# Feed-forward activations: PE transposes replaced by VectorE block transposes and a trip through memory, in a one-core trunk layer

## The chip, the cores and the metric

One core of a Trainium2 chip runs the whole program. The metric is the device time of one launch in microseconds (us); smaller is better. The engines are named as the profile names them: PE (TensorE), ACT (ScalarE), DVE (VectorE), POOL (GpSimd) and SP (SyncE, which here only issues DMAs). SBUF is the working memory, PSUM the accumulators that PE writes.

## The reference

One layer on 256 tokens with width 2048: a norm, an input projection, two mixers (an RWKV-7 recurrence and a gated delta rule), an output projection with a residual, and a gated feed-forward with width 5632. The change touches the feed-forward alone:

```python
x = x + y @ w_out[l]
h = rms_norm(x, ffn_norm_w[l])
x = x + (jax.nn.silu(h @ ffn_w_gate[l]) * (h @ ffn_w_up[l])) @ ffn_w_down[l]
return rms_norm(x, final_norm_w)
```

Everything is float32.

## The kernel before, in words

**Numbers in two halves.** A float32 product is made of three passes of a faster format: each operand is split into a rounded high part and the remainder (`wh` and `wl` for weights, the two halves of `h` for activations), and the passes are high x high, high x low, low x high. ACT makes the high part by a copy (L197 for weights, L241 for activations), DVE the low part by a subtraction (L198, L242).

**The feed-forward by units.** The 44 column blocks of the feed-forward are taken four at a time: eleven units, numbered 0, 4, 8 to 40 after their first block. For each unit there is a *gate* (`gate`, 128 token rows by 512 columns for both halves of the tokens, 96 matmuls, L1065), an *up* of the same size, and two halves of a *down* (`down`, 48 matmuls each, L1142). Gate and up leave their result with tokens on the partitions (`sg`, two tiles of 128 x 512, product at L1084). Down needs the activations with features on the partitions, so they are turned: `turn` does it with eight PE transposes of 128 x 128 into two PSUM tiles (L1097) and then splits these into `h`.

**Order of a unit.** In the loop over units c and the next one c1, the kernel writes gate(c1), down(c, 0), up(c1), down(c, 1); the transposes of c1 stand in the middle of down(c, 1). So `h` of c1 is ready one gate ahead of its use in down(c1, 0).

**Weights.** Every 512 KB of weights is one `load_split` (L179): SP issues the DMA into one of three `raw` buffers, ACT and DVE split it in two halves of 512 columns into one of two `wh` and two `wl` buffers, and PE uses it in 12 matmuls. A gate or an up has eight such loads, a half of a down four. The last unit's down weights come early through `raw_end` and the `wend` places.

**What sets the order.** The code is written in program order, with the feed of the matmuls marked as high priority, and a scheduler with a timeline of its own makes one list of instructions for each engine; each engine then goes through its list in order. `together` ties instructions into a given order. A DMA signals its landing on one of eight semaphores, which are handed out in turn; a DMA whose semaphore is still in use waits for that earlier DMA to land.

Of the kernel before, what the change touches and what calls it, by code (L numbers as in the profile page):

```python
# [17 lines left out]
P = 128  # L18
# [31 lines left out]
def trunk_kernel(ctx, tc, xT, vecs, fnw, w_up, a_up, g_up, w_in, w_ab, w_out, w_gu, w_dn, out):  # L50
# [9 lines left out]
    def hi():  # L60
        return tc.high_priority(offset=HI)
# [81 lines left out]
    class Side:  # L143
# [4 lines left out]
        def step(self):  # L148
            if self.cond is not None:
                if not self.cond():  # L150
                    return False
                self.cond = None
            try:
                self.cond = next(self.gen)
            except StopIteration:
                self.done = True
                side.remove(self)
            return True
# [8 lines left out]
            assert any([g.step() for g in list(side)])  # L167


    first = []  # L170

    def load_split(src, by_k=False, whole=False):

        with hi():
            if first:
                raw = first.pop(0)
            else:
                raw = wp.tile([P, 1024], F32, tag="raw", name="raw", bufs=RAW)
                SY.dma_start(out=raw.rearrange("p (c f) -> p c f", c=4) if by_k else raw, in_=src)  # L179
            wh = wp.tile([P, 1024], F32R, tag="wh", name="wh", bufs=WH)  # L180
            wl = wp.tile([P, 1024], F32R, tag="wl", name="wl", bufs=WL)
            both = [(wh[:, h * 512:h * 512 + 512], wl[:, h * 512:h * 512 + 512]) for h in range(2)]
            if whole:
                split(wh, wl, raw)
                return both
            it = iter(both)
            return halves_of(raw, lambda: next(it), by_k)
# [51 lines left out]
    def split(hi_ap, lo_ap, src, scale=None):  # L239
        if scale is None:  # L240
            S.activation(hi_ap, src, AF.Copy)  # L241
            V.tensor_tensor(lo_ap, src, hi_ap, ALU.subtract)  # L242
        else:
            S.activation(hi_ap, src, AF.Copy, scale=scale)
            V.scalar_tensor_tensor(lo_ap, src, scale, hi_ap, ALU.mult, ALU.subtract)
# [825 lines left out]
    def gate(c0, beside=None):  # L1071
        banks = gate_up(c0, 0, beside=beside)
        sg = [fp.tile([P, 512], F32, tag="tg", name="sg", bufs=2) for _ in range(2)]
        with hi():
            for tb in range(2):
                S.activation(sg[tb], banks[tb], AF.Silu, scale=rstd2[:, tb:tb + 1])
        last_gate[0] = sg[1]
        return sg

    def up(c0, sg, tag="pb"):  # L1080
        banks = gate_up(c0, 1, tag)
        with hi():
            for tb in range(2):
                V.scalar_tensor_tensor(sg[tb], banks[tb], rstd2[:, tb:tb + 1], sg[tb], ALU.mult, ALU.mult)  # L1084
        return sg

    def turn(c0, sg, before=()):

        h = act.tile([P, 4, 2 * T], F32R, tag="act", name=f"h{c0}")
        ps, ms = [], []  # L1090
        for b in range(2):
            ps.append(mps("psT", ("mr", "mc", "mg")[nbank[0] % 3]))
            nbank[0] += 1
            for i in range(2):
                for tb in range(2):
                    o = i * T + tb * P
                    ms.append(PE.transpose(ps[b][:, o:o + P], sg[tb][:, (2 * b + i) * P:(2 * b + i) * P + P], ident))  # L1097
        together([*before, *ms])
        for b in range(2):
            with hi():  # L1100
                p3, hs = ps[b].rearrange("p (i t) -> p i t", i=2), slice(2 * b, 2 * b + 2)
                split(h[:, hs, 0:T], h[:, hs, T:], p3)
        return h

    nbank = [0]

    def wend_slots():

        one = ["lw", "SB", "sq2", "bk", "i3"] + ["kt", "rt"] * 2 + ["vt"] * 4
        bufs = {"kt": 2, "rt": 2, "vt": 4}  # L1110

        def places():
            x2w = rp.tile([P, 8, 512], F32R, tag="AT1", name="wend")
            for i in range(8):
                yield x2w[:, i, :]
            w = act.tile([P, 4, 2 * T], F32R, tag="act", name="wend")
            for i in range(4):
                yield w[:, i, :]
            w = rp.tile([P, 2, 512], F32R, tag="Yt", name="wend")
            yield w[:, 0, :]  # L1120
            yield w[:, 1, :]
            for t in one:
                yield rp.tile([P, 512], F32R, tag=t, name="wend", bufs=bufs.get(t, 1))
            for i in range(6):
                yield fp.tile([P, 512], F32R, tag=("wend", "sq2")[i // 4], name="wend", bufs=(4, 2)[i // 4])
        g = places()
        return lambda: (next(g), next(g))
# [35 lines left out]
            S.copy(acc[:, tb, (q0 + q) * 512:(q0 + q) * 512 + 512], ps[q])  # L1163

    sg = gate(units[0], turn_x2)
    h = turn(units[0], up(units[0], sg, "mg"))

    for c, c1 in zip(units, units[1:]):
        sg = gate(c1)
        down(c, h, 0)  # L1170
        up(c1, sg)
        ahead = []
        down(c, h, 1, lambda m: ahead.append(turn(c1, sg, [m])))
        h = ahead[0]


    n = 4
# [110 lines left out]
```

## Time and profile before

| | |
|---|---|
| median of 3 runs | 1256.41 us (1255.57 to 1258.25) |
| the profiled execution's own time | 1257.04 us |
| its span, first to last instruction | 1255.3 us |
| PE busy | 1231.5 us, 98% of the span |
| DVE, ACT busy | 835.0 us (67%), 650.4 us (52%) |
| feed-forward gate and up matmuls (L1065, high weights) | 1408 matmuls, 377.4 us |
| PE transposes of the activations (L1097) | 88, eight for each of eleven units |
| DMA queue of SP | 171328 packets, 222.19 MB, 60.7% of 16 engines |

Rows of the profile read like this: line, engine, operation, what is written from what, the shapes, how many, then busy time and the mean duration of one, then how long the engine sat idle just before and what ended that idle time. For matmuls the busy time overlaps from one to the next. The chain of waits is followed back from the last instruction; in its list in order of time each piece has its start and its length in us. For a DMA issue the duration is the time for which SP is occupied; the time to landing runs from the start of the issue.

### The profile page before, as it was taken

The page shows a single profiled execution, that of the slowest core. Times are in us where ns is not written, and L with a number is a line of the kernel's source. Part 1 is how long each engine was busy: PE and PEld are TensorE (multiplying, and loading weights), DVE is VectorE, ACT ScalarE, POOL GpSimd, SP SyncE. Part 2 cuts the span into 40 slices and gives each one's busy share as a digit, 9 for nine tenths or more (in the row PEclk, how much of TensorE's full clock was granted, in tenths as well). Part 3 has the DMA queues.
Part 4 walks back from the last instruction along what each step waited for, and adds up shares of the span by engine and source line. Part 5 has one row for each costly group of instructions (what it writes and reads, how often), then busy time and mean ns, then how long its engine had stood idle before and what let it go on. Part 6 is the DMA issues. An engine that isn't in the chain of part 4 may idle for free.

```text
span 1255.3 us, 21107 instructions
## 1 busy us (share of the span) xinstructions
PE 1231.5 (98%) x8122; PEld 1084.1 (86%) x8122; DVE 835.0 (67%) x1634; ACT 650.4 (52%) x1199; POOL 17.0 (1%) x63
## 2 busy tenths in 40 slices
PE   7999999999999999999999999999999999999997
PEld 6999999999999989888888888888888888878886
DVE  7987887978966867555556555655656565665554
ACT  6665555666545556664444444444444444454443
POOL 3000000000000000000000000000000000000000
PEclk9999999999999999999999999999999999999999
DMA  6555666575573445676666666766666766676651
GB/s 232 167 168 178 162 170 157 168 183 142 179 231 118 135 165 188 167 209 191 190 191 195 188 190 194 197 188 197 186 187 189 194 187 195 202 239 192 194 150 67
DMA packets 175701, 226.68 MB, mean 181 GB/s; under 512 B 52272, under 2 KB 144560, under 8 KB 175344
## 3 DMA queue, kind: packets, MB, share of 16 engines
q1 hardware_dynamic: 171328, 222.19, 60.7%
q10 hardware_dynamic: 4128, 2.10, 0.6%
q8 instruction: 64, 1.05, 0.4%
q0 software_dynamic: 144, 1.05, 0.2%
q14 instruction: 37, 0.30, 0.1%
HBM read 218.75 MB, written 4.46 MB: 178 GB/s over the span
## 4 chain that ended last, share of the span: by engine, by line
PE 86%; DMA 5%; DVE 5%; ACT 1%; SPq 1%; issue 1%; DVEq 0%; ACTq 0%
PE psq L1065 36%; PE psd L1142 17%; PE psb L215 16%; PE psb L218 8%; DMA raw_end<-in_w_dn 2%; DVE wl L242 1%; PE psT L1097 1%; DMA raw<-in_w_in 1%; DMA A_r<-sA 1%; DMA sA<-AT 1%; PE psd L1193 1%; PE psd L1191 1%; PE psd L1192 1%; PE ps_A L480 1%; DVE wend L198 1%
## 5 line engine op out<-in xcount | busy, mean ns | idle before, releaser
L198 DVE TENSOR_TENSOR wl<-raw,wh 128x512 fp32r<-128x512 f32 x524 | 341.5, 694 | 273.0 <-ACT wh L197 271.0
L197 ACT ACTIVATE wh<-raw 128x512 fp32r<-128x512 f32 x524 | 302.0, 625 | 363.2 <-PE psq L1065 203.9
L1065 PE MATMUL psq<-wh,x2s 128*128 128x512 f32 x1408 | 377.4, 390 | 0.4 <-ACT wh L197 0.4
L1065 PEld LDWEIGHTS psq<-wh,x2s 128*128 128x128 f32 x1408 | 263.7, 188 | 55.6 <-ACT wh L197 1.0
L1065 PE MATMUL psq<-wl,x2s 128*128 128x512 f32 x704 | 217.2, 389 | 0.0
L215 PE MATMUL psb<-xs,wh 128*128 128x256 f32 x816 | 207.3, 288 | 7.6 <-ACT wh L197 6.1
L218 PE MATMUL psb<-xs,wh 128*128 128x256 f32 x816 | 206.9, 287 | 0.0
L1142 PE MATMUL psd<-wh,h 128*128 128x512 f32 x640 | 203.5, 391 | 1.0 <-ACT wh L197 1.0
L241 ACT ACTIVATE wh<-raw 128x1024 fp32r<-128x1024 f32 x128 | 135.3, 1057 | 86.6 <-PE psb L218 71.2
L215 PEld LDWEIGHTS psb<-xs,wh 128*128 128x128 f32 x816 | 157.3, 193 | 9.1 <-ACT wh L197 6.1
L242 DVE TENSOR_TENSOR wl<-raw,wh 128x1024 fp32r<-128x1024 f32 x128 | 155.9, 1218 | 10.8 <-ACT wh L241 10.7
L218 PEld LDWEIGHTS psb<-xs,wh 128*128 128x128 f32 x816 | 157.4, 193 | 1.5 <-issue 0.7
L1065 PEld LDWEIGHTS psq<-wl,x2s 128*128 128x128 f32 x704 | 132.0, 188 | 27.5
L1142 PEld LDWEIGHTS psd<-wh,h 128*128 128x128 f32 x640 | 119.1, 188 | 26.3 <-ACT wh L197 2.3
L215 PE MATMUL psb<-xs,wl 128*128 128x256 f32 x816 | 127.8, 287 | 2.2 <-DVE wl L198 1.2
L1142 PE MATMUL psd<-wl,h 128*128 128x512 f32 x320 | 124.6, 389 | 0.0
L215 PEld LDWEIGHTS psb<-xs,wl 128*128 128x128 f32 x816 | 110.4, 193 | 4.5 <-DVE wl L198 2.0
L1142 PEld LDWEIGHTS psd<-wl,h 128*128 128x128 f32 x320 | 60.1, 188 | 12.7
L218 PE MATMUL psb<-ys,wh 128*128 128x256 f32 x256 | 64.5, 288 | 2.5 <-DVE ys L242 2.5
L215 PE MATMUL psb<-ys,wh 128*128 128x256 f32 x256 | 64.7, 289 | 0.2 <-ACT ys L241 0.2
L218 PEld LDWEIGHTS psb<-ys,wh 128*128 128x128 f32 x256 | 50.1, 196 | 2.8 <-DVE ys L242 2.7
L1150 DVE TENSOR_TENSOR acc<-acc,psd 128x512 f32<-128x512 f32 x80 | 49.5, 681 | 1.8 <-PE psd L1142 1.8
(312 smaller groups left out, 1014.2 us busy)
## 6 DMA issues: line engine op xcount, KB each, us to landing
raw<-in_w_gu SPq DMA_DIRECT2D x176, 512.0 KB, 4.8
raw<-in_w_in SPq DMA_DIRECT2D x99, 512.0 KB, 3.9
raw<-in_w_dn SPq DMA_DIRECT2D x80, 512.0 KB, 4.2
raw<-in_w_out SPq DMA_DIRECT2D x32, 512.0 KB, 3.5
raw_end<-in_w_dn SPq DMA_DIRECT2D x8, 512.0 KB, 4.4
xraw<-in_xT SPq DMA_DIRECT2D x8, 256.0 KB, 6.3
x<-in_xT SPq DMA_DIRECT2D x1, 2048.0 KB, 9.7
raw<-in_w_ab SPq DMA_DIRECT2D x2, 512.0 KB, 6.1
```

The costliest lines, as they stand in the source:

```text
L197: S.activation(oh, src, AF.Copy)
L198: V.tensor_tensor(ol, src, oh, ALU.subtract)
L215: PE.matmul(ps[:, 0:T], w, rt[:, ri, 0:T], start=(first and k == 0 and not low), stop=(last and k == 7 and low == 1))
L218: PE.matmul(ps[:, 0:T], w, rt[:, ri, T:], start=False, stop=False)
L241: S.activation(hi_ap, src, AF.Copy)
L242: V.tensor_tensor(lo_ap, src, hi_ap, ALU.subtract)
L480: PE.matmul(psA[h][:, ch, :], bk[hr, ch].rearrange("p a t -> p (a t)"), ar[hr, p, ch].rearrange("p a t -> p (a t)"), start=True, stop=True)
L1065: last = PE.matmul(banks[tb], t[:, ri, o + tb * P:o + tb * P + P], w, start=(k == 0 and o == 0 and w is wh), stop=(k == KB - 1 and w is wl))
L1097: ms.append(PE.transpose(ps[b][:, o:o + P], sg[tb][:, (2 * b + i) * P:(2 * b + i) * P + P], ident))
L1142: m = PE.matmul(banks[tb * 2 + cg], st, parts[cg][w], start=(i == 0 and w == 0 and st is hh), stop=(i == n - 1 and st is hl))
L1150: V.tensor_tensor(acc[:, tb, cs], acc[:, tb, cs], banks[tb * 2 + cg], ALU.add)
L1191: PE.matmul(ps, hh, wh, start=(i == 0), stop=False)
```

## The change

For units 0 to 36 the activations no longer go through PE. A new function, `turn_far`, transposes each `sg` tile in blocks of 32 x 32 on DVE (`V.transpose`) into `tn`. What is then still wrong is where the blocks lie. `tn` is stored to a tensor in memory, `sH`, with two DMAs of 256 KB, and read back with sixteen DMAs of 32 KB, each for 32 partitions and one column block, in runs of 128 bytes, into the low half of `h`; then ACT and DVE split it in place. The three steps (store, read, split) are called from the next unit's gate, after its second, fourth and sixth weight load; the sixteen reads are tied behind the last weight load issued by then and to each other. Unit 40, the last, keeps the PE transposes, in the middle of down as before. One small buffer (tag `i3`) moves from the end's places to `tn`.

```diff
-    first = []
+    first, loads = [], []
...
-                SY.dma_start(out=raw.rearrange("p (c f) -> p c f", c=4) if by_k else raw, in_=src)
+                loads.append(SY.dma_start(out=raw.rearrange("p (c f) -> p c f", c=4) if by_k else raw, in_=src))
...
+    def turn_far(c0, sg):
+
+        tn = []
+        for tb in range(2):
+            tn.append(rp.tile([P, 512], F32, tag=("i2", "i3")[tb], name=f"tn{tb}"))
+            with hi():
+                V.transpose(tn[tb], sg[tb])
+        h = act.tile([P, 4, 2 * T], F32R, tag="act", name=f"h{c0}")
+        sH = dr.tile([2, 4, 32, 512], F32, name=f"sH{c0}")
+        raw = h[:, :, T:].bitcast(F32)
+        blocks = sH.rearrange("b a r (i q c) -> q r i (b a) c", i=4, q=4)
+
+        def step(i, last):
+            with hi():
+                if i == 0:
+                    for tb in range(2):
+                        SY.dma_start(out=sH[tb].rearrange("a r f -> (a r) f"), in_=tn[tb])
+                elif i == 1:
+                    together([loads[-1]] + [SY.dma_start(out=raw[q * 32:q * 32 + 32, j].rearrange("r (a c) -> r a c", c=32),
+                                                         in_=blocks[q][:, j]) for q in range(4) for j in range(4)])
+                elif i == 2:
+                    split(h[:, :, 0:T], h[:, :, T:], raw)
+        return h, step
...
-        one = ["lw", "SB", "sq2", "bk", "i3"] + ["kt", "rt"] * 2 + ["vt"] * 4
+        one = ["lw", "SB", "sq2", "bk"] + ["kt", "rt"] * 2 + ["vt"] * 4
...
-    h = turn(units[0], up(units[0], sg, "mg"))
+    h, step = turn_far(units[0], up(units[0], sg, "mg"))
 
     for c, c1 in zip(units, units[1:]):
-        sg = gate(c1)
+        sg = gate(c1, step)
         down(c, h, 0)
         up(c1, sg)
-        ahead = []
-        down(c, h, 1, lambda m: ahead.append(turn(c1, sg, [m])))
-        h = ahead[0]
+        if c1 != units[-1]:
+            ahead = [turn_far(c1, sg)]
+            down(c, h, 1)
+        else:
+            ahead = []
+            down(c, h, 1, lambda m: ahead.append((turn(c1, sg, [m]), None)))
+        h, step = ahead[0]
```

The order of the instructions on the engines moves with it. On SP, in the changed kernel, from the four loads of a down half of unit 4 on, through the gate in which unit 8's activations are read back (`sH_8118` is their place in memory, `h_8117` the tile they are read into):

```order
L179 DMA raw<-in_w_dn 128x1024 x4
L1121 DMA sH_8118<-tn_8113 128x512
L179 DMA raw<-in_w_gu 128x4x256
L1121 DMA sH_8118<-tn_8115 128x512
L179 DMA raw<-in_w_gu 128x4x256 x3
L1123 DMA h_8117<-sH_8118 32x8x32 x7
L179 DMA raw<-in_w_gu 128x4x256
L1123 DMA h_8117<-sH_8118 32x8x32 x5
L179 DMA raw<-in_w_gu 128x4x256
L1123 DMA h_8117<-sH_8118 32x8x32 x4
L179 DMA raw<-in_w_gu 128x4x256 x2
```

Before, the same stretch was four loads of the down half and eight of the gate with nothing between them. Now the two stores stand ahead of the gate's first and second load, and the reads behind its fourth, fifth and sixth. A part of the same list again, with what each DMA waits for (`DMAHW2` is one of the eight landing semaphores, `DVE` the raw buffer coming free), from the gate's fifth load on:

```order
L179 DMA raw<-in_w_gu 128x4x256 [waits DMAHW2_49,DVE_49]
L1123 DMA h_8117<-sH_8118 32x8x32 [waits DMAHW3_49]
L1123 DMA h_8117<-sH_8118 32x8x32 [waits DMAHW4_49]
L1123 DMA h_8117<-sH_8118 32x8x32 [waits DMAHW5_49]
L1123 DMA h_8117<-sH_8118 32x8x32 [waits DMAHW6_49]
L1123 DMA h_8117<-sH_8118 32x8x32 [waits DMAHW7_49]
L179 DMA raw<-in_w_gu 128x4x256 [waits DMAHW0_49,DVE_49]
L1123 DMA h_8117<-sH_8118 32x8x32 [waits DMAHW1_49]
L1123 DMA h_8117<-sH_8118 32x8x32 [waits DMAHW2_49]
```

Each waits for the DMA eight places back: the fifth load for the fourth load's landing, and the fourteenth read, the last row, for the fifth load's.

On DVE, before, from the product of unit 8's up to the end of the next gate's first split (`h_8135` is that unit's tile, read from PSUM):

```order
L1084 SCALAR_TENSOR_TENSOR sg<-psq,rstd_6748,sg 128x512 x2
L198 TENSOR_TENSOR wl<-raw,wh 128x512 x6
L242 TENSOR_TENSOR h_8135<-psT,h_8135 128x2x256 x2
L198 TENSOR_TENSOR wl<-raw,wh 128x512 x2
L1150 TENSOR_TENSOR acc<-acc,psd 128x512 x4
```

and now:

```order
L1084 SCALAR_TENSOR_TENSOR sg<-psq,rstd_6748,sg 128x512 x2
L198 TENSOR_TENSOR wl<-raw,wh 128x512
L1111 STREAM_TRANSPOSE tn_8113<-sg 128x512
L198 TENSOR_TENSOR wl<-raw,wh 128x512
L1111 STREAM_TRANSPOSE tn_8115<-sg 128x512
L198 TENSOR_TENSOR wl<-raw,wh 128x512 x6
L1174 TENSOR_TENSOR acc<-acc,psd 128x512 x4
L198 TENSOR_TENSOR wl<-raw,wh 128x512 x8
L242 TENSOR_TENSOR h_8117<-h_8117 128x4x256
L198 TENSOR_TENSOR wl<-raw,wh 128x512 x16
```

The two transposes follow the product, between half splits of weights. The split of `h`, once in down, now stands in the gate: the eight half splits ahead of it are those of the gate's second to fifth load, and the first behind it is the sixth load's. ACT has the same place for its part:

```order
L1076 ACTIVATE sg<-psq,rstd_6748 128x512 x2
L197 ACTIVATE wh<-raw 128x512 x38
L241 ACTIVATE h_8117<-h_8117 128x4x256
L197 ACTIVATE wh<-raw 128x512 x10
L1076 ACTIVATE sg<-psq,rstd_6748 128x512 x2
```

Before, this list had 28 weight halves, two splits of `h` from PSUM, and 20 halves; now 38 halves, one split of `h`, and 10.

## The prediction

> **What bounds the kernel now.** First the page: busy shares and the chain of work that ended last.
>
> ```profile
> PE 1231.5 (98%) x8122; PEld 1084.1 (86%) x8122; DVE 835.0 (67%) x1634; ACT 650.4 (52%) x1199; POOL 17.0 (1%) x63
> PE 86%; DMA 5%; DVE 5%; ACT 1%; SPq 1%; issue 1%; DVEq 0%; ACTq 0%
> ```
>
> PE is busy 98% of the span and holds 86% of the chain. So the feed-forward stage runs at the pace of its matmuls, and work taken off PE there is worth its full time, as long as PE gets its operands. The chain in order of time, over one unit, shows how little else is in it:
>
> ```profile
> 681.36 5.44 PE psd L1142 x24
> 686.80 0.87 PE psT L1097 x8
> 687.68 5.47 PE psd L1142 x24
> 693.15 21.76 PE psq L1065 x96
> 714.91 10.88 PE psd L1142 x48
> ```
>
> A gate takes 21.76 us for 96 matmuls and 8 weight loads, so one load feeds 12 matmuls, 2.72 us. The eight transposes of a unit take 0.87 us, as bare PE time. The gate that starts at 693.15 is my sample; its loads are numbered 0 to 7 and times are given from its start. Load 5 is wanted at 5 x 2.72 = 13.60.
>
> What supplies PE is one strict line: SP issues a load into one of three raw buffers, ACT rounds it, DVE subtracts.
>
> ```profile
> 692.45 0.37 SPq L179 DMA_DIRECT2D raw<-in_w_gu  x1
> 696.05 0.37 SPq L179 DMA_DIRECT2D raw<-in_w_gu  x1
> 697.44 0.37 SPq L179 DMA_DIRECT2D raw<-in_w_gu  x1
> ...
> raw<-in_w_gu SPq DMA_DIRECT2D x176, 512.0 KB, 4.8
> ```
>
> These are the issues of loads 3, 4 and 5: -0.70, +2.90 and +4.29. An issue occupies SP for 0.37, and 4.8 us after its start the load has landed.
>
> **What is removed.** Ten units lose their transposes (the eleventh keeps them): 10 x 0.87 = 8.7 us off PE. Their split from PSUM gives way to one of the same bytes from SBUF, on ACT and DVE, which have idle time there. That is the whole possible gain.
>
> **What is added on DVE and in memory.** Two block transposes a unit. The nearest row is half as wide:
>
> ```profile
> L364 DVE STREAM_TRANSPOSE tn_r<-st_r x2: 445/446/446, 187.0 to 271.8; 128x256 f32<-128x256 f32 x2
> ```
>
> At twice the elements an estimate is 0.7 us (between 0.45 and 0.89). They stand between the two halves of a weight split, on a DVE that is busy 67%; the split they delay is the one for the second load of a down stage, wanted some two microseconds later, so I cost them at nothing; without that cover it would be 0.7 a unit. The two stores take the same bytes as one weight load, and have from the end of the up stage until load 3, some 11 us, to land. The sixteen reads move 512 KB in runs of 128 bytes:
>
> ```profile
> A_r<-sA SPq DMA_DIRECT2D x8, 128.0 KB, 3.7
> ...
> sG<-gates SPq DMA_DIRECT2D x1, 512.0 KB, 3.7
> ...
> Bd_r<-sA SPq DMA_DIRECT2D x8, 32.0 KB, 3.4
> ```
>
> Bd_r is the very form of a read, 32x8x32 with 128-byte runs from memory. Four times as many runs (A_r) land only 0.3 us later, so the small packets are cheap: I give the DMA engines nothing.
>
> **What is added on SP, and what queues behind it.** The price is in the issue:
>
> ```profile
> L540 SPq DMA_DIRECT2D Bd_r<-sA x8: 592/607/857, 131.4 to 214.8; - x8
> DMA to landing us min/median/max: 2.9/3.4/4.1
> ...
> 132.99 1.89 SPq L540 DMA_DIRECT2D Bd_r<-sA  x3
> ...
> 212.57 2.81 SPq L540 DMA_DIRECT2D Bd_r<-sA  x4
> ...
> L543 SPq DMA_DIRECT2D ar<-sX_r x8: 432/489/2197, 185.2 to 271.7; - x8
> ```
>
> Seven in 4.70 us: 0.67 each, gaps included. The other small reads of 32 partitions (L543) have 0.49; that is the lower bound, and 0.70 the upper. I take 0.67, since the shapes are the same. The order of SP puts seven reads behind load 3, five behind load 4, four behind load 5. Worked through from load 3's issue, which nothing moves:
>
> - Reads 1 to 7 from -0.3 to +4.4. Load 4 goes at 4.4 instead of 2.9, lands at 9.2; wanted at 10.88, ACT needs 0.62: no stall.
> - Reads 8 to 12 from 4.8 to 8.15. Load 5 goes at 8.15 instead of 4.29, lands at 12.95.
> - Reads 13 to 16 from 8.55; the last is issued at 10.56 and lands 3.4 later, at **13.96** (2.9 to 4.1: 13.5 to 14.7).
>
> ACT and DVE take their work in order, and on both the split of h stands ahead of the split of load 5. So load 5, landed at 12.95, waits for read 16.
>
> ```profile
> L198 DVE TENSOR_TENSOR wl<-raw,wh 128x512 fp32r<-128x512 f32 x524 | 341.5, 694 | 273.0 <-ACT wh L197 271.0
> L197 ACT ACTIVATE wh<-raw 128x512 fp32r<-128x512 f32 x524 | 302.0, 625 | 363.2 <-PE psq L1065 203.9
> ...
> L241 ACT ACTIVATE wh<-raw 128x1024 fp32r<-128x1024 f32 x128 | 135.3, 1057 | 86.6 <-PE psb L218 71.2
> ...
> L242 DVE TENSOR_TENSOR wl<-raw,wh 128x1024 fp32r<-128x1024 f32 x128 | 155.9, 1218 | 10.8 <-ACT wh L241 10.7
> ```
>
> ACT's split of h ends at 13.96 + 1.06 = 15.02, its first half of load 5 at 15.64: PE idles 15.64 - 13.60 = 2.0. DVE ends h's low part at 15.02 + 1.22 = 16.24 and load 5's at 16.93, while PE's first four matmuls end at 15.64 + 0.91 = 16.55: another 0.4. **The stall is 2.4 us a unit** where 0.87 is saved. Load 6 (issued 11.6, landed 16.4) is split in time, and the line recovers.
>
> Eight units have this pattern. Unit 32 has ten reads ahead of load 4 and six behind it: load 4 goes at 6.4, is split at 11.8 (0.9 late), load 5 goes at 10.8, is split at 16.2, 1.7 more: 2.6. Unit 0 has no down stage between its up and the next gate, and all sixteen reads ahead of load 6:
>
> ```profile
> 559.68 1.41 DVE L1084 SCALAR_TENSOR_TENSOR sg<-psq,rstd,sg 128x512 f32<-128x512 f32 x2 [0.15 <-PE psq L1065]
> ...
> 567.79 0.37 SPq L179 DMA_DIRECT2D raw<-in_w_gu  x1
> ...
> 564.37 18.16 PE psq L1065 x80
> ```
>
> DVE's order there is product, half split, transpose, half split, transpose: 561.09 + 2 x (0.69 + 0.7) = 563.9. The store lands 3.7 later, at 567.6, and sixteen reads take 10.7: load 6 goes at 578.3 instead of 567.79, lands 4.8 later and is split at 583.7. PE wants it at 582.53 - 0.87 - 5.44 = 576.2: 7.5 us.
>
> **What a stall does to the clock.** The windows view, three stretches of one period of the clock's record:
>
> ```profile
> 460.65:464.06 3.41, 0.88 (x6) 0.44 (x4) 3.41 (x5) 2.19 (x4) 0.00 (x0) 1.00 0.42 154
> 464.06:467.47 3.41, 3.20 (x15) 3.20 (x16) 1.96 (x4) 0.23 (x1) 0.69 (x1) 0.50 0.03 11
> 23.74:27.15 3.41, 2.20 (x16) 2.00 (x17) 3.41 (x4) 2.12 (x4) 2.74 (x3) 1.00 0.44 154
> ```
>
> A period with 2.53 us of idle was followed by one at half clock, a loss of 1.7 us; one with 1.21 idle was not. A stall of 2.0 lies wholly in one period in 41% of cases and else is cut in two; with the threshold unknown between 1.21 and 2.53 I let half the stalls pay: 0.85 a unit. The Trainium skill, TensorE: Matmul & The Clock Gate, section "Part 1: The HAM clock gate", halves the clock only after at least one idle window of about 3.4 us; the trace differs, since 2.53 idle of 3.41 sufficed there, but only a run can tell for these stalls. By that rule the middle units would pay nothing, and the sum would be rival B's.
>
> **Sum.** Eight units 8 x (2.4 + 0.85) = 26.0; unit 32 2.6 + 0.85 = 3.5; unit 0 7.5 + 1.7 = 9.2; less 8.7: +30.0. The profiled execution took 1257.04 (span 1255.3), 0.6 above the median of the runs, 1256.41. So 1257.0 + 30.0 = **1287 us**.
>
> **Rivals.**
>
> A, faster: the reads hide. The point is a last landing at 13.60 - 0.62 - 1.06 = 11.9 or earlier. Then only the 8.7 stays, 1248 us. For it: the DMA engines have room, and the issue may be shorter than Bd_r's. Against it: at 0.49 a read too, each DMA waits for its semaphore's last user eight issues back, load 4 for load 3 and read 14 for load 4; load 4 cannot go before -0.7 + 4.8 = 4.1, read 14 not before 4.1 + 4.8 = 8.9, and read 16, issued at 9.9, lands at 13.3. The Trainium skill, DMA: Bandwidth & Descriptors, section "Issuing engines are not separate DMA queues", holds that the time to initiate is usually small relative to the DMA itself; one read's 0.61 against 3.4 agrees, sixteen in a row don't, and by the rule's letter rival A would come out.
>
> B, the clock holds through stalls of this length, and only unit 0 pays: 30.0 - 9 x 0.85 = +22.3, 1279 us.
>
> C, late landings: 4.1 instead of 3.4 makes the stall 3.1, and every one then pays 1.7: 8 x 4.8, unit 32 2.6 + 1.7 = 4.3, unit 0 8.2 + 1.7 = 9.9, less 8.7: +44, 1301 us. For it: the weight loads land at 4.8 here, later than elsewhere.
>
> D, short issue (0.49): by the times of A ACT's first half of load 5 is ready at 13.3 + 1.06 + 0.62 = 14.98, a stall of 1.4 + 0.4 = 1.8 with the clock left alone; unit 32 has none, since its load 4 goes at 4.6; unit 0 loses 7.5 - 16 x 0.18 = 4.6: 14.4 + 4.6 - 8.7 = +10.3, 1267 us.
>
> **How the numbers follow.** Forecast 0.50, B 0.17, D 0.13, C 0.10, A and what lies near break-even 0.10. The forecast's own range is 1276 to 1297. The range to hold 8 in 10 takes in B and D and most of C: 1264 to 1305. Faster by over 0.2% (2.5 us, about what a measurement of this kernel can tell from no change) is A without its break-even part, 0.07; within 0.2% 0.03; slower 0.90.
>
> **What would show it.** Right: read issues of about 0.6 on SP; load 5 issued some 8 us after its gate's start; ACT idle ahead of the split of h with a DMA of h as releaser; PE idle of about 2 us ahead of load 5 once a unit and of about 7 in the second gate; half clock behind some of them. Wrong: reads issued in 0.4 or less, or landings ahead of ACT's reaching h; PE's idle time unchanged from before; or a stall at the transposes of DVE instead.

## The result, and the profile after

The changed kernel takes 1309.14 us (median of 4 runs, 1306.58 to 1312.36), the kernel before 1256.24 beside it: a ratio of 1.0416, 95% interval 1.0390 to 1.0443. It is slower by some 53 us; 1287 was predicted, in a range that ended at 1305. The profiled execution took 1306.58 with a span of 1304.9, that of before 1257.04 with 1255.3.

Busy shares and the chain of waits, of the changed kernel:

```profile
PE 1241.3 (95%) x8042; PEld 1080.6 (83%) x8042; DVE 845.7 (65%) x1644; ACT 649.4 (50%) x1189; POOL 16.9 (1%) x63
PE 68%; DMA 18%; DVE 8%; issue 2%; ACT 2%; SPq 2%; ACTq 0%; DVEq 0%
```

PE has lost 18 points of the chain (86% before), most of them to DMAs. The 80 transposes are gone, and yet PE's busy time rose from 1231.5 to 1241.3: some of its time was at half clock.

The windows view says where the time came. First the kernel before, then the changed one, in four stretches: from the first gate to the gate of unit 8; from there seven units to the gate of unit 36; from there to the gate of unit 40; and the rest. A row has the stretch, its length, busy time of PE, PEld, DVE, ACT and POOL with instructions, the granted clock, the DMA share and GB/s.

```profile
511.60:626.80 115.20, 115.20 (x538) 95.96 (x537) 63.54 (x102) 59.53 (x104) 0.00 (x0) 1.00 0.68 192
626.80:1090.11 463.31, 463.31 (x2074) 384.18 (x2073) 268.31 (x424) 209.89 (x366) 0.00 (x0) 1.00 0.67 191
1090.11:1158.95 68.84, 67.45 (x298) 54.36 (x297) 43.83 (x72) 34.70 (x62) 0.00 (x0) 1.00 0.73 222
1158.95:1255.30 96.35, 88.51 (x405) 73.44 (x403) 50.59 (x85) 39.98 (x78) 0.00 (x0) 0.99 0.47 137
```

```profile
510.80:635.50 124.70, 116.36 (x522) 96.08 (x521) 64.30 (x102) 58.48 (x101) 0.00 (x0) 0.96 0.68 189
635.50:1133.03 497.53, 472.39 (x2018) 383.59 (x2016) 272.86 (x427) 208.66 (x358) 0.00 (x0) 0.98 0.71 192
1133.03:1205.19 72.16, 67.59 (x290) 53.24 (x288) 47.35 (x76) 35.66 (x63) 0.00 (x0) 1.00 0.80 229
1205.19:1304.90 99.71, 89.39 (x405) 73.21 (x403) 51.67 (x86) 40.90 (x79) 0.00 (x0) 0.97 0.51 139
```

A unit's activations are read back in the next gate, so the second stretch holds the reads of units 4 to 28 (and the turning of 8 to 32). Seven units took 497.53 where they took 463.31: 71.08 a unit instead of 66.19. With the 0.87 of transposes given back, what was added is:

| part | predicted | measured |
|---|---|---|
| units 4 to 28, seven | 7 x 3.25 = 22.8 | 34.22 + 7 x 0.87 = 40.3 |
| unit 36 | 3.25 | 3.4 |
| unit 32 | 3.45 | 3.32 + 0.87 = 4.2 |
| unit 0 | 9.2 | 9.50 + 2 x 0.87 = 11.2 |
| transposes saved | -8.7 | -8.7 |

That is 50.4, and with a start that was 0.8 earlier the 49.6 by which the span grew. The prediction had 30.0, so it lacked 20.4, and 17.5 of that (40.3 - 22.8) is in the seven middle units.

In one such gate, which starts at 635.50, the chain in order of time reads:

```profile
635.05 6.16 DMA raw<-in_w_gu
...
641.27 0.39 SPq L179
...
641.71 5.43 DMA h<-sH
...
647.54 3.70 DMA h<-sH
...
651.39 1.06 ACT h L241
```

and SP's issues are:

```profile
635.52 3.41 SPq L1123 DMA_DIRECT2D h<-sH  x7
641.27 0.39 SPq L179 DMA_DIRECT2D raw<-in_w_gu  x1
641.71 2.49 SPq L1123 DMA_DIRECT2D h<-sH  x5
644.29 0.40 SPq L179 DMA_DIRECT2D raw<-in_w_gu  x1
644.73 3.26 SPq L1123 DMA_DIRECT2D h<-sH  x4
```

Seven reads take 3.41, 0.49 each. Then SP stands idle until load 3, issued at 635.05, has landed at 641.21, and only then issues load 4: its semaphore was load 3's. Read 14 waits for load 4 in the same way, inside the 3.26, and reads 15 and 16 for reads 8 and 9, which land right behind load 4. SP's waits between 635 and 650:

```profile
SPq L179 <- DMA raw<-in_w_gu: 2.3, 1, 2.3
...
SPq L1123 <- DMA raw<-in_w_gu: 1.2, 1, 1.2
```

The last read goes at 647.54 and lands at 651.24, 15.74 after the gate's start; the split of h follows, then load 5, which had landed at 650.37, 6.08 after its issue. PE idled 2.54 for it (650.48 to 653.02), and 0.93 before that for load 4. The waits between 600 and 1200, before and after (total, times, longest):

```profile
ACT wh L197 <- DMA raw<-in_w_gu: 20.1, 9, 3.4
...
PEld psq L1065 <- ACT wh L197: 1.0, 2, 0.8
```

```profile
ACT wh L197 <- DMA raw<-in_w_gu: 75.1, 33, 5.5
PEld psq L1065 <- ACT wh L197: 34.5, 18, 4.5
...
ACT h L241 <- DMA h<-sH: 13.7, 5, 3.7
```

Landing times, and the new reads' occupation of SP (ns, min/median/max):

```profile
raw<-in_w_gu SPq DMA_DIRECT2D x176, 512.0 KB, 5.2
sH<-tn SPq DMA_DIRECT2D x20, 256.0 KB, 4.1
h<-sH SPq DMA_DIRECT2D x160, 32.0 KB, 4.5
```

```profile
L1123 SPq DMA_DIRECT2D h<-sH x160: 302/449/1810, 568.9 to 1216.6; - x160
```

The clock, in the period of the stall and the one behind it:

```profile
650.84:654.25 3.41, 1.20 (x4) 0.67 (x4) 1.77 (x3) 2.21 (x4) 0.00 (x0) 1.00 0.72 230
654.25:657.66 3.41, 3.30 (x8) 2.62 (x9) 1.86 (x4) 1.37 (x3) 0.00 (x0) 0.50 0.56 165
```

Six of the seven middle units have such a half-clock period (the others start at 725.93, 797.62, 869.29, 1009.24 and 1080.92), 1.7 us each.

### The profile page after: what moved, and what is told of

Read it like the earlier page. It is cut to its first block, busy times and chain, and to the rows that moved or that the text cites. A ratio compares the mean times of both kernels' runs of the same rounds, so it can differ in the third digit from the quotient of the medians.

```text
span 1304.9 us, 21264 instructions
## 1 busy us (share of the span) xinstructions
PE 1241.3 (95%) x8042; PEld 1080.6 (83%) x8042; DVE 845.7 (65%) x1644; ACT 649.4 (50%) x1189; POOL 16.9 (1%) x63
## 3 DMA queue, kind: packets, MB, share of 16 engines
q1 hardware_dynamic: 217728, 232.68, 63.4%
## 4 chain that ended last, share of the span: by engine, by line
PE 68%; DMA 18%; DVE 8%; issue 2%; ACT 2%; SPq 2%; ACTq 0%; DVEq 0%
PE psq L1065 26%; PE psb L215 16%; PE psd L1166 11%; DMA raw<-in_w_gu 9%; PE psb L218 8%; DMA h<-sH 4%; DVE wl L198 2%; DVE wl L242 1%; SPq L1123 1%; DMA raw_end<-in_w_dn 1%; DMA raw<-in_w_in 1%; ACT wh L197 1%; PE ps_A L480 1%; PE psd L1221 1%; PE psd L1220 1%
## 5 line engine op out<-in xcount | busy, mean ns | idle before, releaser
L1065 PE MATMUL psq<-wh,x2s 128*128 128x512 f32 x1408 | 388.2, 398 | 37.7 <-ACT wh L197 37.6
L1065 PEld LDWEIGHTS psq<-wh,x2s 128*128 128x128 f32 x1408 | 268.0, 192 | 102.6 <-ACT wh L197 46.7
L1065 PE MATMUL psq<-wl,x2s 128*128 128x512 f32 x704 | 222.9, 398 | 2.5 <-DVE wl L198 1.5
```

Of the source, the lines that this page charges most:

```text
L1065: last = PE.matmul(banks[tb], t[:, ri, o + tb * P:o + tb * P + P], w, start=(k == 0 and o == 0 and w is wh), stop=(k == KB - 1 and w is wl))
```

## The experiments

Theories. **1**: the stall is made where the split of h, in the list of ACT and DVE ahead of load 5's, waits for the last read. **2**: the weight loads themselves are late, because the reads stand on SP's line: their issue, their packets in the same queue, the turns of the semaphores. **3**: the clock adds 1.7 to a stall. **4**: packets of 128 bytes slow the DMA engines. A stop is a stretch in which PE stands idle. All ratios are against the kernel before, run beside each; "a unit" is the mean of the seven middle units (66.19 before, 71.08 changed).

| kernel | median, us | ratio, 95% interval | a unit |
|---|---|---|---|
| changed | 1309.1 | 1.0416 (1.0390 to 1.0443) | 71.08 |
| late split | 1282.4 | 1.0200 (1.0174 to 1.0227) | 68.17 |
| reads on POOL, split behind load 6 | 1261.0 | 1.0026 (1.0012 to 1.0040) | 65.41 |
| reads on POOL, split within load 5 | 1311.3 | 1.0432 (1.0415 to 1.0450) | 70.26 |
| traffic only | 1286.8 | 1.0232 (1.0204 to 1.0260) | 67.90 |
| traffic only, an eighth of the packets | 1272.5 | 1.0116 (1.0100 to 1.0132) | 67.37 |
| unit 0 on PE | 1294.4 | 1.0300 (1.0268 to 1.0331) | 70.85 |
| reads 6, 5, 5 | 1304.9 | 1.0389 (1.0372 to 1.0407) | 70.07 |
| reads 6, 5, 5 and late split | 1277.4 | 1.0177 (1.0152 to 1.0203) | 67.69 |
| spread over SP, late split, unit 0 on PE | 1257.7 | 0.9995 (0.9983 to 1.0008) | 66.04 |
| POOL, units 0 and 32 on PE | 1251.2 | 0.9944 (0.9927 to 0.9961) | 65.66 |
| ACT, units 0 and 32 on PE | 1277.3 | 1.0160 (1.0141 to 1.0179) | 68.95 |

### The split of h moved behind load 7

```diff
-                elif i == 2:
-                    split(h[:, :, 0:T], h[:, :, T:], raw)
+                elif i == 3:
+                    for a, b in zip(list(halved), (S.activation(h[:, :, 0:T], raw, AF.Copy),
+                                                   V.tensor_tensor(h[:, :, T:], raw, h[:, :, 0:T], ALU.subtract))):
+                        together([a, b])
```

(`halved` holds the two instructions of the last weight half.)

> The split of h on ACT and DVE is moved from ahead of load 5's split to behind load 7's; the stores, the sixteen reads and their places on SP stay. Theory 1 (the stall is made where the split of h waits for the last read, ahead of load 5): load 5 landed at 650.37 in the changed kernel and was split from 652.36, so some 1.9 us of each middle unit's idle time go, and with them the half-clock periods behind them (1.7 each, six of them): 9 x 1.9 + 6 x 1.7 = 27, so about 1282 us; PE idle per unit 1.5 to 2.5 instead of 2.5 to 4.7, no half clock in the middle units. Theory 2 (the weight loads themselves come late, because SP issues them behind the reads and they land beside them): loads 4, 5 and 6 still land at the same times, so PE idles almost as long, in smaller pieces: 1300 us or more, the half-clock periods still there.

1282.4, what theory 1 said. In the seven middle units no half-clock period is left:

```profile
632.34:1109.52 477.18, 463.45 (x2018) 376.79 (x2016) 273.11 (x427) 207.91 (x358) 0.00 (x0) 1.00 0.73 200
```

A unit fell by 2.9 to 68.17; the transposes' absence alone would make 65.32. So the place of the split made half of a unit's loss. The other half, 2.85, is loads that come late by themselves, as theory 2 has it: PE now stops three times in a gate, ahead of loads 4, 5 and 6 (0.20, 0.62 and 0.66 in the gate that starts at 632.34), 1.96 of idle a unit.

A stop costs more than the idle time that the profile shows. PE's rows around the second one:

```profile
646.00 0.61 PE L1064 MATMUL psq<-wl,x2s 128*128 128x512 f32 x2
647.23 1.19 PE L1064 MATMUL psq<-wh,x2s 128*128 128x512 f32 x4 [0.62 <-ACT wh L197]
```

At full pace two matmuls take 0.45 (21.76 / 96 each) before the next can start, but the last one's end is shown 0.16 later; and the four behind the stop take 1.19, where such a group elsewhere takes 1.07. So each stop costs 0.28 more than its idle time, and three of them, with the 1.96, make 2.80 of the 2.85.

### The reads on POOL's queue

```diff
-                    together([loads[-1]] + [SY.dma_start(out=raw[q * 32:q * 32 + 32, j].rearrange("r (a c) -> r a c", c=32),
-                                                         in_=blocks[q][:, j]) for q in range(4) for j in range(4)])
+                    together([G.dma_start(out=raw[q * 32:q * 32 + 32, j].rearrange("r (a c) -> r a c", c=32),
+                                          in_=blocks[q][:, j]) for q in range(4) for j in range(4)])
```

> Only the sixteen reads of each unit move, from SP's queue to POOL's, which has no work there: they no longer stand ahead of loads 4 to 6 on SP, share no queue with them and leave SP's eight landing semaphores alone. Theory 2 (SP's line is what delays loads 4 to 6): the loads go out as before the change, the last read is in before load 5 is wanted, all stalls go, unit 0's 8.3 us too: 1248 to 1258 us. Theory 4 (the 128-byte packets of the reads slow down the DMA engines for whatever loads run beside them): the loads still land 5 to 6 us after their issue instead of 4.8 and the reads late, so ACT still waits for the last read: 1275 to 1300 us. Theory 1 (the place of the split alone) says about 1290: the last read still comes as late as POOL can issue it.

1261.0: three us above theory 2's interval, and a unit takes 65.41, nothing lost in the middle. But this run changed two things, since the scheduler also put the split of h behind load 6's. Of ACT, in the gate that starts at 630.55:

```profile
645.34 1.16 ACT L197 ACTIVATE wh<-raw 128x512 fp32r<-128x512 f32 x2 [1.41 <-DMA raw<-in_w_gu]
646.40 1.05 ACT L241 ACTIVATE h<-h 128x1024 fp32r<-128x1024 f32 x1
```

POOL needs longer for a read than SP (584 ns against 449), and its reads land later after their issue, 5.8 against 4.5:

```profile
L1123 POOL DMA_DIRECT2D h<-sH x160: 582/584/624, 568.5 to 1170.8; - x160
...
h<-sH POOLq DMA_DIRECT2D x160, 32.0 KB, 5.8
```

The last read came in 15.25 after the gate's start, hardly earlier than before (15.74). Beside these reads the loads landed no sooner after their issue: loads 4, 5 and 6 took 6.26, 7.28 and 6.92. But they had been issued 3.64, 4.84 and 7.77 after the gate's start, where the changed kernel issued them at 5.77, 8.79 and 12.59, and PE did not stop for them. What the loads had lost on SP was their turn, more than their speed.

A third thing moved with the queue. On SP's queue the profile counts 272 packets for a read, 256 runs of 128 bytes and 16 more (217728 packets in the changed kernel less 174208 here, by 160 reads); on POOL's it counts 32 (5264 less 144, by 160). So this run alone doesn't part the place on SP from the small packets; the run with an eighth of each read, below, bounds the packets' part. The next run put the split back.

### The reads on POOL's queue, the split of h back at load 5

```diff
+                if beside and (kk % 2 or (q, kk) == (1, 0) and c0 != units[0]):
+                    beside(2 * q + kk // 2 if kk % 2 else 9, last)
...
+                elif i == 9:
+                    got[:] = [S.activation(h[:, :, 0:T], raw, AF.Copy), V.tensor_tensor(h[:, :, T:], raw, h[:, :, 0:T], ALU.subtract)]
+                    for a, b in zip(halved[-1], got):
+                        together([a, b])
+                elif i == 2:
+                    for a, b in zip(got, halved[-2]):
+                        together([a, b])
```

(Step 9 is called behind load 4's matmuls; it ties the split of h behind load 4's second half and ahead of load 5's first.)

> The reads on POOL's queue for all ten units (1261 us, where the split of h had also moved: behind load 6's split), and the split of h put back to load 5, between its two halves, on ACT and DVE. In the run with POOL the last read landed at 645.80 for a gate that started at 630.55, 15.25 after it, no earlier than in the changed kernel (15.74). Theory 1 (a split of h ahead of a weight half that PE wants sooner than the last read lands): ACT ends h at 15.25 + 0.05 + 1.06 = 16.4, the second half of load 5 at 17.0, where PE wants it at 13.60 + 1.36 = 14.96: 2.0 of idle and 0.4 more from DVE, in nine units, and half-clock periods behind up to all of them (1.7 each): 1261 + 22 = 1283 to 1298 us. Theory 2 (SP's line is what costs, and the split can stand anywhere once the reads are off it): 1261 us.

1311.3: all of the gain is gone, and 13 us more than theory 1's upper end. ACT waits again:

```profile
648.70 0.63 ACT L197 ACTIVATE wh<-raw 128x512 fp32r<-128x512 f32 x1 [1.39 <-DMA raw<-in_w_gu]
651.97 1.06 ACT L1127 ACTIVATE h<-h 128x1024 fp32r<-128x1024 f32 x1 [2.63 <-DMA h<-sH]
```

In the units 4 to 28 PE idles 2.8 to 4.2 at this place, five of the seven have a half-clock period, and unit 0 (9.7 of idle) and unit 32 (78.7 long) are worse than in the changed kernel. One half of load 5 stands ahead of the split of h and one behind it, as the expectation said; but PE stops after 60 matmuls of the gate, five loads of 12, so what stood behind was the first half, which PE wants 1.36 sooner than the second. That is part of the 13 us, and it makes the place, for PE, that of the changed kernel, which stops after 60 as well.

With the two runs before, the square is full: split early, SP or POOL: 1.0416 and 1.0432; split late, SP or POOL: 1.0200 and 1.0026. With the split early the intervals of the two queues overlap; with it late, the queue of the reads is worth 1.7%, some 21 us. Theory 2 as the sole cause falls, and so does theory 1. The late places are not quite the same (behind load 7 on SP, behind load 6 on POOL), and no run holds one against the other.

### The traffic alone

All eleven units are turned by PE as before the change; the DVE transposes, stores and reads run at their places, into a spare tile that nothing reads.

```diff
-        h = act.tile([P, 4, 2 * T], F32R, tag="act", name=f"h{c0}")
+        raw = fp.tile([P, 4, T], F32, tag="spare", name=f"spare{c0}")
...
-                elif i == 2:
-                    split(h[:, :, 0:T], h[:, :, T:], raw)
...
-        if c1 != units[-1]:
-            ahead = [turn_far(c1, sg)]
-            down(c, h, 1)
+        step = turn_far(c1, sg) if c1 != units[-1] else None
+        ahead = []
+        down(c, h, 1, lambda m: ahead.append(turn(c1, sg, [m])))
...
```

> All of the trip through memory runs (transposes on DVE, two stores, sixteen reads, at the same places), but what is read lands in a spare tile that nobody reads, and all eleven units are turned by PE as before the change. So nothing waits for the reads but what stands behind them on SP. Theory 1 (the wait of the split of h makes the stall): the time of before plus unit 0's late load 6 (8.3 of idle and 2.8 of clock) and the 0.9 of load 4 in nine units: 1256 + 11 + 8 = about 1275 us. Theory 2 (weight loads late by SP's line): 1256 + 50 + 9 less little, 1295 us or more.

1286.8, between the two expectations. A unit took 67.90, 1.71 over before, with no wait for a read left in it: that is the price of the traffic for the loads. It is less than the 2.85 of the late split. In the gate that starts at 634.52 load 3 landed 4.95 after its issue and PE did not stop for load 4; in the late split load 3 took 5.69 and PE stopped. Why is not shown. Unit 0's idle was 7.84.

### The same with an eighth of each read

```diff
-                    together([loads[-1]] + [SY.dma_start(out=raw[q * 32:q * 32 + 32, j].rearrange("r (a c) -> r a c", c=32),
-                                                         in_=blocks[q][:, j]) for q in range(4) for j in range(4)])
+                    together([loads[-1]] + [SY.dma_start(out=raw[q * 32:q * 32 + 32, j, 0:32],
+                                                         in_=blocks[q][:, j, 0]) for q in range(4) for j in range(4)])
```

> The run in which all units are turned by PE and the reads go to a spare tile (1287 us), with each of the sixteen reads cut to an eighth: 32 packets of 128 bytes instead of 256. The issues, their places on SP and their semaphores stay. If what makes the loads late is the issuing of sixteen DMAs and the turns of the semaphores: 1280 to 1287 us, unit 0's idle still about 8. If it is the packets that queue between the loads: they are an eighth, so most of the 30 us go: 1258 to 1270 us, the gate's loads land 4.8 us after their issue again.

1272.5, outside both expectations. In the middle units little changed, 67.37 after 67.90: of the 1.71 that the reads cost there, 0.53 went with the packets and 1.18 stayed with the issues and the turns. SP, in the gate that starts at 629.00:

```profile
633.01 0.39 SPq L179 DMA_DIRECT2D raw<-in_w_gu  x1
```

Load 4 again goes late, 4.01 after the start and not 2.90. Half of the gain, 7 us, is in unit 0, and that cannot be read as packets: an eighth of a read needs only the first of the two stores, and of the sixteen reads twelve stood ahead of load 5 and four between it and load 6, where all sixteen had stood between the two. PE stopped for 2.02 and 0.90 there, not for 7.84.

### Unit 0 back on PE

```diff
-    h, step = turn_far(units[0], up(units[0], sg, "mg"))
+    h, step = turn(units[0], up(units[0], sg, "mg")), None
```

> Unit 0 alone goes back to PE's transposes; the other nine units stay as changed. All theories: unit 0's idle of 8.3 us and 2.8 of half clock go, 0.87 of PE work comes back: 1309 - 10.3 = about 1299 us. If it gains less than 7, unit 0's stall has another cause than its sixteen reads ahead of load 6.

1294.4. The stretch from the first gate to unit 8's is 114.2 long after 124.7, 10.5 less where 10.3 was expected. The spans of the two profiles are 12.1 apart (1292.8 and 1304.9), so 1.6 lies elsewhere in them; the rest of the 14.8 between the medians is that the profiled execution of the changed kernel was 2.6 below its median. Unit 0's own chain in the changed kernel shows what it paid for:

```profile
562.82 6.06 DMA sH<-tn
...
576.46 0.45 SPq L1123
...
577.01 5.99 DMA raw<-in_w_gu
...
583.78 8.36 PE psq L1065 x24
```

Store, sixteen issues, load: each ends in the next, and PE stands still for 8.34 us, from 575.45 to 583.78, where the last row begins.

### Six reads behind load 3 instead of seven

With six, load 4's semaphore is that of load 2, and the wait for load 3 falls to the seventh read. (In a second kernel the same with the late split.)

```diff
-                    together([loads[-1]] + [SY.dma_start(out=raw[q * 32:q * 32 + 32, j].rearrange("r (a c) -> r a c", c=32),
-                                                         in_=blocks[q][:, j]) for q in range(4) for j in range(4)])
+                    got[:] = [loads[-1]] + [read(x) for x in range(16 if c0 == units[0] else 6)]
+                    together(list(got))
+                elif i == 3 and c0 != units[0]:
+                    together([got[-1], loads[-2]])
                 elif i == 2:
+                    if c0 != units[0]:
+                        got[:] = [got[-1], loads[-2]] + [read(x) for x in range(6, 11)] + [loads[-1]] + [read(x) for x in range(11, 16)]
+                        together(list(got))
```

(`read(x)` issues read x of the sixteen; `got` holds the list so far.)

> As the changed kernel, but in the units 4 to 32 the reads stand 6, 5 and 5 behind loads 3, 4 and 5 instead of 7, 5 and 4, so that load 4's place eight DMAs back is load 2, long landed, and not load 3; the seventh read takes the wait for load 3 instead. If load 4 was late by its semaphore's turn (in the changed kernel it went out at 641.27, 0.06 us after load 3's landing): it goes out some 2.8 us earlier, the 0.6 to 0.9 of idle ahead of load 4 go, the last read is issued about 1.2 us earlier: eight units gain 1 to 2 us each, and a half-clock period or two may go with it: 1288 to 1301 us. If load 4 was held up by the seven issues or by its raw buffer: no change, 1305 to 1311 us.

> The same order of the reads (6, 5, 5) with the split of h behind load 7's, to be held against the run with the late split alone (1282 us), where no half-clock period is left and load 4's idle of 0.5 to 1.1 us a unit stands alone. If it is the semaphore's turn: 8 x 0.6 to 1.1, 1273 to 1278 us. If not: 1282 us.

In the gate that starts at 634.02 load 4 now goes 3.15 after the start, not 5.77:

```profile
633.58 0.37 SPq L179 DMA_DIRECT2D raw<-in_w_gu  x1
634.05 2.91 SPq L1121 DMA_DIRECT2D h<-sH  x6
637.17 0.39 SPq L179 DMA_DIRECT2D raw<-in_w_gu  x1
639.17 2.37 SPq L1121 DMA_DIRECT2D h<-sH  x5
```

So the semaphore's turn did hold load 4 (one read less ahead of it accounts for 0.49 of the 2.62), and the idle ahead of it is gone. What it is worth is small: 1.0 a unit with the early split, 0.5 with the late one. The first median, 1304.9, lies between the two expectations, a hair below "no change"; the second, 1277.4, is where the semaphore's turn would put it. Both ratios' intervals overlap those of the kernels they are held against, so the gain in total is not established. Load 5 stays late in both.

### Versions that keep the trip through memory

Everything on SP, spread over the gate, the split behind load 7's, unit 0 on PE:

(Of the edit, the reads alone; `i` is the step, four of them in a gate.)

```diff
+                    together([loads[-1]] + [SY.dma_start(out=raw[i * 32:i * 32 + 32, j].rearrange("r (a c) -> r a c", c=32),
+                                                         in_=blocks[i][:, j]) for j in range(4)])
```

> All DMAs stay on SP, but the sixteen reads are spread over the gate (2, 2, 4, 4 and 4 behind the loads 1, 2, 3, 5 and 7), the split of h stands behind load 7's, and unit 0 is turned by PE. If the length of SP's line is what costs (sixteen issues of 0.45 to 0.49 and the turns of the landing semaphores, 8 us a unit however they are spread, in a gate of 21.76 us with eight loads of 0.37), spreading should let every load go in time: about 1250 us. If what costs is that a load and reads beside each other land late (5 to 6 us instead of 4.8), each load still meets it and small idle pieces stay, 0.5 to 1.5 us a unit: 1254 to 1262 us. If the first reads, which wait for the second store's landing ahead of load 2, hold up SP: above 1262 us, with the idle time ahead of load 2 or 3.

1257.7, ratio 0.9995, within the second expectation: most of the 0.87 a unit is saved and spent again (66.04, where 65.32 was possible), and the stretch with unit 32's reads takes 72.75 where it took 68.84. Loads still land 5.3 after their issue, and SP waits for the stores, 32 us between 600 and 1200, mostly without PE's idling for it.

The reads on POOL, and units 0 and 32 on PE:

```diff
-    h, step = turn_far(units[0], up(units[0], sg, "mg"))
+    h, step = turn(units[0], up(units[0], sg, "mg")), None
...
-        if c1 != units[-1]:
+        if c1 not in (units[-3], units[-1]):
```

> The reads on POOL's queue as in the run before, and the trip through memory only for the units 4 to 28 and 36; units 0, 32 and 40 are turned by PE. With the reads on POOL the middle units took 65.3 us each, as long as before the change less 0.87, and what was lost was unit 0 (5.24 us of idle and 1.7 of half clock ahead of its first down) and unit 32, whose trip meets the early loads of the last down (5.8 of idle where it was 1.4). If SP's line was the whole cause in the middle units, eight units now keep their 0.87 and nothing is lost: 1256 - 7 = 1249 us. If the trip costs something that the middle units only hide, or the loss around unit 32 does not go with its trip: 1253 to 1258 us.

1251.2, ratio 0.9944, interval 0.9927 to 0.9961: faster than the kernel before by 0.6%, the only version here that is, and between the two expectations. The seven units, with unit 32's transposes among them:

```profile
626.55:1086.14 459.59, 459.35 (x2025) 378.74 (x2024) 275.83 (x431) 210.44 (x361) 63.20 (x110) 1.00 0.75 208
```

The same with the reads issued by ACT, between its weight halves (the edit is `S.dma_start` for `G.dma_start`):

> The kernel with the reads on POOL's queue for units 4 to 28 and 36 (1251 us, ratio 0.994), with the reads issued by ACT instead, between its weight halves. If all that matters is that the reads are off SP's line: 1251 us again. If the issues cost their engine what they cost SP (0.45 to 0.49 each, sixteen, in groups of three and four ahead of weight halves that PE waits for): each group makes the next load's high half 1.5 to 2 us late, where ACT has slack of 0.1 to 2 us ahead of a load: 1252 to 1262 us.

1277.3, worse than the second expectation. What had not been foreseen is SP's own wait, between 600 and 1200:

```profile
SPq L179 <- DMA h<-sH: 97.7, 27, 6.6
```

ACT's reads and SP's weight loads take turns on the same eight landing semaphores, so a load on SP waits for a read on ACT; POOL's reads, in the run before this one, made no load of SP wait. Which part of the 26 us is this and which is ACT's own issuing was not told apart.

## Why the prediction was wrong, step by step

The mechanism was the predicted one: the split of h, ahead of load 5's split, waits for the last read, and the clock adds to the stall. The step that failed is the landing of the weight loads. The sum took 4.8 us for each; with reads behind them loads 3, 4 and 5 took 6.16, 5.41 and 6.08. Through the turns of the semaphores this made load 4 and the last read late, and so the split. Of the 20.4 us that the sum lacked, the longer stall in the seven middle units is 8.3 (3.59 of idle a unit where 2.4 was said), half clock more often 4.3, the edges of the stops 4.9, unit 0 2.0 and units 32 and 36 0.9.

- **PE is the bound, and 10 x 0.87 is the whole gain**: right. Units on POOL's queue take 65.41, 0.78 less than before.
- **DVE's transposes, 0.7 each, at no cost**: right. They took 698 to 706 ns, and no wait of PE ends in one.

```profile
L1111 DVE STREAM_TRANSPOSE tn<-sg x20: 698/703/706, 560.9 to 1197.4; 128x512 f32<-128x512 f32 x20
```

- **An issue of a read takes 0.67**: wrong; 0.49 with its gap, the lower bound. By itself this would have led to rival D, 1267, further off: the two errors had opposite signs, and that 1287 came no further from 1309 is luck.
- **"Load 4 goes at 4.4 ... no stall"**: wrong, and this is where the failed step shows first. It went at 5.77 and PE idled 0.93 for it. The working for rival A had named the cause, load 4 waiting for load 3's landing, but with 4.8 for that landing; it took 6.16 with seven reads behind it in the queue. Then read 14 waited for load 4's landing, 5.41 after its issue. Put both into rival D's times: last read issued at 9.9 + 1.36 + 0.61 = 11.9; it was 12.04. The term that was mis-sized is the landing of a weight load beside reads.
- **"Load 5 goes at 8.15 ..., lands at 12.95"**: 8.79 and 14.87. ACT needs 0.62 for its first half, so load 5 would have been late for PE's 13.60 (14.53 with the stop for load 4) without any split of h ahead of it; the late split shows that loss by itself.
- **The last read lands at 13.96, 3.4 after its issue**: 15.74, 3.70 after its issue; the lateness is the issue's, 1.48 of 1.78.
- **The split of h ahead of load 5 makes the stall, 2.0 and 0.4**: right in place, shown by the two moves of the split; 2.54 in the sample, and with load 4's idle 3.59 a unit (497.53 - 472.39, by 7).
- **Load 6 is "split in time, and the line recovers"**: wrong as soon as the split is out of the way. With the late split PE stops for load 6 too, and a unit still has 2.85 over 65.32.
- **The clock, half of the stalls at 1.7**: six of seven pay, 1.46 a unit and not 0.85. With 3.59 and 1.46 of the 5.76 a unit accounted for, 0.7 is left: the edges of the stops, up to 0.28 each as worked out for the late split, at 2.9 stops a unit. The sum had no term for them.
- **Unit 0, 7.5 and 1.7**: 8.34 and 2.8, the half clock lying over PE's first two periods of work. The store took 6.06 instead of 3.7, the load 5.99 instead of 4.8; the issues took less. Errors of both signs.
- **The DMA engines at nothing (theory 4)**: wrong in part: 0.53 of 1.71 a unit went with seven eighths of the packets.
- **Rivals**: C had late landings and the clock at every stall, and its 1301 was nearest, though it put the lateness on the last read; it belonged to the loads, and through the semaphores to SP's line. D had the issue right and the landings wrong. A and B fall.

The clock's condition can now be drawn closer. Three pairs of neighbouring periods, from the changed kernel, from the one with POOL's reads and the early split, and from the one with ACT's reads. In the first two pairs the first period holds the idle time, and the second has the answer in its clock; in the third one stall lies across the border of both:

```profile
865.88:869.29 3.41, 1.77 (x7) 1.17 (x8) 2.43 (x3) 2.27 (x4) 0.00 (x0) 1.00 0.63 202
869.29:872.70 3.41, 3.41 (x10) 2.63 (x9) 1.90 (x3) 1.99 (x4) 0.00 (x0) 0.50 0.62 168
```

```profile
859.17:862.58 3.41, 1.57 (x7) 0.95 (x6) 0.69 (x1) 1.20 (x2) 0.00 (x0) 1.00 0.88 236
862.58:866.00 3.42, 2.27 (x9) 1.55 (x10) 2.96 (x4) 2.00 (x4) 0.00 (x0) 1.00 0.15 33
```

```profile
769.60:773.01 3.41, 2.40 (x11) 1.67 (x9) 0.29 (x1) 0.00 (x0) 0.00 (x0) 1.00 1.03 228
773.01:776.42 3.41, 1.94 (x8) 1.61 (x9) 1.94 (x4) 2.31 (x4) 0.00 (x0) 1.00 0.67 125
```

1.64 of idle in one period was followed by half clock; 1.84 in another was not; and a stall of 2.48, cut by a period's border into 1.01 and 1.47, left the clock alone (the period behind 776.42 is at full clock too). Over all periods at full clock from 505 us on, in the thirteen profiles: 33 with over 1.86 of idle, and half clock behind every one; 2786 with under 1.58, and behind none; and of the 18 between, behind seven. So the border is not sharp, it lies between 1.6 and 1.9 us in one period of 3.41, and where a stall falls decides as much as its length. Ahead of the feed-forward, with other matmuls, one period with 1.14 of idle was followed by half clock as well (275.24 in the kernel of 1251 us). The Trainium skill, TensorE: Matmul & The Clock Gate, section "Part 1: The HAM clock gate", asks for at least one idle window of some 3.4 us; the runs differ: about half a window sufficed.

The Trainium skill, DMA: Bandwidth & Descriptors, section "Issuing engines are not separate DMA queues", holds that issuing from several engines saves only the sequencer's time to initiate. The trace agrees for the reads, which were in at 15.25 from POOL and at 15.74 from SP; but that sequencer's time, and the place in the semaphores' turns, was worth some 21 us to the loads behind.

## What to carry to other kernels

When a helper's work is put into the lists of engines that prepare the next weights, ask which instruction stands behind it there, and when that one is wanted: here the place of one split cost 27 to 50 us, the queue of its reads 21 or nothing. Many small DMAs on a queue of large loads can cost more than their issue: in this program each took a turn of the landing semaphores, and a load waited for whatever was eight places back, with a landing time that had grown by what was queued beside it. So a landing time has to be taken from a row with the same neighbours: the same read took 3.70 to 6.03 us in the sample gate, and 1.8 to 2.3 in the gate of unit 0's reads, where hardly a load was under way.

## What the runs showed of the hardware that was not expected

- In the feed-forward the granted clock halved behind a 3.41 us period with over 1.86 us of idle, and never behind one with under 1.58 (rows above).
- A 512 KB load with seven 32 KB reads behind it landed 6.16 us after its issue, where the median before was 4.8.
- The same read was 272 packets on SP's queue and 32 on POOL's, as the profile counts them.
- An issue occupied POOL for 584 ns, SP for 449 and ACT for some 460 for the same read.

Of this program and not of the chip: its DMAs issued by ACT and by SP shared the turns of the eight landing semaphores (97.7 us of waits of SP's loads for ACT's reads); those issued by POOL had others.
